# A hybrid decoder block on one core: four more gate blocks by seven products, and all modulation rows out of the retention stage

## The chip, the cores and the metric

The kernel runs on one core of a Trainium2 chip. The metric is the device time of one execution in microseconds. The number before is the median of three runs; a profile of one more execution is read beside it.

## The reference, cut

One decoder block, sequence 1024, width 1024, all in float32. A conditioning vector gives six rows of 1024 modulation values (`c` through SiLU, times `w_ada`). The normed and modulated input goes through one wide projection, and two token mixers run on it side by side; a squared-ReLU MLP follows.

```
mod = silu(c) @ w_ada + b_ada                 # sh1, sc1, g1, sh2, sc2, g2
h = modulate(rms_norm(x, norm1_g), sh1, sc1)
proj = h @ w_in                               # rq, rk, rv, rg, 9 attention parts, 2 gates
ro = retention(rotary(rq), rotary(rk), rv)    # 4 heads, chunks of 128, carried state
ro = group_norm(ro) * gn_g + gn_b
ret_out = (silu(rg) * ro) @ w_ret_out
att_out = dilated attention (3 groups of 4 heads) @ w_att_out
x = x + g1 * ((sigmoid(gate_a) * ret_out + sigmoid(gate_b) * att_out) @ w_o)
x = x + g2 * mlp(modulate(rms_norm(x, norm2_g), sh2, sc2))
return rms_norm(x, norm_f_g)

# retention, one chunk of one head
s = (q @ k.T) * inner_decay
o = s @ v + (q @ state) * q_decay
state = state * chunk_decay + (k * k_decay).T @ v
```

The change is about `rg`, the retention's gate: 2048 columns, 512 a head, in four blocks of 128 a head, sixteen in all.

## The kernel before

Every float32 operand is split into a high and a low half of the type fp32r, and each product is three matmuls (`mm3`: high by low, low by high, high by high) of a stationary 128x128 with a moving 128x512. In the profile these are the lines L210, L212 and L214.

**Blocks by seven products.** The projection stage (`queries_keys`) goes through a list of *pairs*, `PAIRS`; a pair is two blocks of 128 output columns. The contraction, the pair and the sequence are each cut in two, and a scheme of seven products in place of eight is run on the quarters (the class `Blocks`, items `ORDER`). Each product is four row blocks by three matmuls: 84 matmuls a pair. Sums of operands and results are made on VectorE. A pair of kind `r` (retention queries and keys) is followed by the rotary step on VectorE; the kinds `a`, `k`, `g` and `s` have no such step: these are the light pairs. Kind `g` are branch gates, kind `s` the retention's gate; their results go through an activation function and out to DRAM. There are 22 pairs, two of them `s`, the last two.

**Blocks by four products.** The other twelve `rg` blocks are computed in the retention stage, as filling for TensorE: `rg_mm(n)` issues n units, one unit being one of eight contraction blocks of an `rg` block, six matmuls. Eight units end a block, and ScalarE evicts it (L709, SiLU, two halves) into a tile of the ring `E` (five buffers). Its PSUM tiles come from a ring of three, and a block takes two. The table `RG` says how many units each chunk issues.

**The retention stage.** One step per chunk, 8 chunks by 4 heads, in an order written out by hand (`chunk`). On TensorE: `kv` (six matmuls, the state's increment; not in a head's last chunk), the chunk's units but one, `sT` (scores of the next chunk) and `kT` (two transposes of its key; none where the next chunk is a head's last), `o` (nine matmuls), `oT` (four transposes of the chunk before's output), one unit. Beside it VectorE updates the state (L749) and makes its low half (L752), ScalarE copies the scores (L655), makes the state's high half (L756) and evicts the transposes `onT` (L686), VectorE takes the statistics of `o` (L777 to L779), GpSimd makes scale and offset from them in three small steps (L780 to L782, the second a power), and ScalarE writes the scaled output `on` (L790, tile `onm`). `ahead(2)` prepares the weights that the next chunk brings: a cast on ScalarE (L200) and a subtraction on VectorE (L201). From head 1 on VectorE also multiplies an earlier head's output by its gate (L693).

All of the chunk's other PSUM tiles (`kv` twice, `sT`, `kT`, `o`, `oT`) come from one ring of five banks, in this order, so that a tile waits for the readers of the tile five places before it:

```
PS["n"] = 8 if single else 5 if ret else 4
...
return PS["p"].tile(list(shape), F32, tag="s", bufs=PS["n"], name=name)
```

**Modulation rows.** The 48 columns of modulation values are products of a 128x1024 weight tile with the broadcast SiLU of `c`, summed along the row on VectorE. Sixteen are made at the start, 22 by `mod_turn` (two turns a row, a turn with each product of the late pairs and of `values`, from pair 16 on), and the last ten as loads of retention steps (`mod_load`, L467): one in each of chunks 3 to 6 of head 0, two in the first chunk of heads 1, 2 and 3, prepared in the chunk before.

Of the kernel before, what the change touches and what calls it, by code (L numbers as in the profile page):

```python
# [11 lines left out]
F32 = mybir.dt.float32  # L12
# [5 lines left out]
P = 128  # L18
D = 1024
S = 1024  # L20
NK = D // P
H = 4
C = 128
NC = S // C
# [116 lines left out]
def block_kernel(ctx, tc, io, stop=None, dbg=None):  # L141
    nc = tc.nc
# [5 lines left out]
    dram = ctx.enter_context(tc.tile_pool(name="dram", bufs=1, space=bass.MemoryType.DRAM))  # L148
# [20 lines left out]
    def ps_rg(name):  # L169
        return PS["p"].tile([P, 512], F32, tag="rg", bufs=3, name=name)  # L170
# [21 lines left out]
    SH1, SC1, G1, SH2, SC2, G2 = (8 * i for i in range(6))  # L192
# [271 lines left out]
    def mod_prep(i):  # L464

        def prep(raw):
            nc.vector.scalar_tensor_tensor(raw, raw, 1.0, cb, op0=ALU.mult, op1=ALU.mult,  # L467
                                           accum_out=mods[:, i:i + 1])
            nc.vector.tensor_add(mods[:, i:i + 1], mods[:, i:i + 1], vec[:, VC_BADA + i:VC_BADA + i + 1])
        return prep  # L470

    def mod_load(i):
        return io["w_ada"][i], mod_prep(i)

    def proj_mm(ps, w, ks=range(NK)):
        outs = ps if isinstance(ps, list) else [ps[:, 0, :], ps[:, 1, :]]
        for k in ks:
            mm3(outs, wk(w, k), hx[k], k == 0, k == NK - 1)
# [36 lines left out]
    def etile(name, dt=F32):  # L515
        return R["p"].tile([P, 1024], dt, tag="E", bufs=5, name=name)
# [66 lines left out]
    hd = {}  # L583
# [109 lines left out]
        nc.vector.tensor_mul(t, t, hd["srg", h, e][:, 512 * hf:512 * hf + 512])  # L693
        queue.dma_start(y_d[h][:, 2 * (i % 2) + hf, e // 2], t)

    RG = (6, 2, 2, 3, 3, 3, 3, 2), (3, 3, 2, 3, 3, 2, 4, 4), (3, 3, 2, 3, 3, 2, 4, 4), (3, 3, 2, 3, 3, 2, 4, 4)

    def rg_mm(n):

        for _ in range(n):  # L700
            if hd.get("rgk", NK) == NK:
                hd["rgk"], hd["rgw"], hd["rgp"] = 0, hd["rgws"].pop(0), [ps_rg(f"rg{i}") for i in range(2)]
            proj_mm(hd["rgp"], hd["rgw"], [hd["rgk"]])
            hd["rgk"] += 1
            if hd["rgk"] == NK:
                i = hd["rgi"] = hd.get("rgi", -1) + 1
                t = hd["srg", i // 3, i % 3] = etile(f"srg{i // 3}{i % 3}")
                for j, ps in enumerate(hd["rgp"]):
                    nc.scalar.activation(t[:, 512 * j:512 * j + 512], ps, AF.Silu)  # L709

    def rg_out(h, c):

        if c == 6:
            hd["srg", h, 3] = etile(f"srg{h}3")
            nc.sync.dma_start(hd["srg", h, 3], srg_d[h])

    def chunk(h, c, ahead, w=None):
        p = R["p"]
# [7 lines left out]
        if g == 0:  # L726
            rg_mm(2)
            s_kt(0)
            rg_mm(2)
# [9 lines left out]
        if g == 0:  # L739
            s_kt(1)  # L740
        rg_mm(1 if g == 0 else RG[h][c] - (g < NG - 1))
        for i, kv in enumerate(kvs):
            if g == 0:
# [46 lines left out]
        nc.scalar.activation(on, po, AF.Identity, scale=gr[:, 1:2], bias=gr[:, 2:3])  # L790
        hd["o", h, c] = on
        rg_out(h, c)

    def wsplit(ap):
        return ap, split_w
# [2 lines left out]
    va_d = [dram.tile([S, 512], F32, name=f"vad{g}") for g in range(3)]  # L798
    aq_d = {(p, g, a): dram.tile([P, S], F32, name=f"aqd{p}{g}{a}") for p in range(2) for g in range(3) for a in range(2)}
    ak_d = {(p, a): dram.tile([P, S], F32, name=f"akd{p}{a}") for p in range(2) for a in range(2)}  # L800
    srg_d = [dram.tile([P, S], F32, name=f"srgd{h}") for h in range(H)]
    h12_d = [dram.tile([P, 2, 512], F32, name=f"h12d{m}") for m in range(4)]
    xn, wa = [], []

# [330 lines left out]
    def sums_of_h(name, ms=range(4)):  # L1135

        for m in ms:
# [18 lines left out]
            if name != "t4":  # L1156
# [7 lines left out]
    a_pairs = [("a", g, p) for p in range(2) for g in range(3)]  # L1164
    g_pairs = [("g", i) for i in range(len(GATES) // 2)]
    k_pairs = [("k", 2, p) for p in range(2)]
    s_pairs = [("s", i) for i in range(H // 2)]
    PAIRS = [{"r": r_pairs, "a": a_pairs, "g": g_pairs, "k": k_pairs, "s": s_pairs}[i].pop(0)
             for i in "rargrarkrargrarkgagass"]
    MOD0 = 16 * len(ORDER) + 4  # L1170
    NA = len(PAIRS)
    OA = {}
# [74 lines left out]
    gate_d = [dram.tile([P, S], F32, name=f"gated{i}") for i in range(16)]  # L1247
    BA = Blocks("qa", XA, ["x"] * 4 + ["wh", "wl"] * 3, lambda kind: True, a_place, a_two, a_temps, a_out)

    NV = 22  # L1250
    turn = {"n": 0, "i": 0}

    def mod_turn():

        turn["n"] += 1
        while turn["i"] < NV + 2 and turn["n"] > 2 * turn["i"]:
            i = turn["i"]
            turn["i"] += 1
            t = cs[:, i % 2]
            if i > 1:  # L1260
                m = G1 + i - 2
                nc.vector.scalar_tensor_tensor(t, t, 1.0, cb, op0=ALU.mult, op1=ALU.mult, accum_out=mods[:, m:m + 1])
            if i < NV:
                nc.sync.dma_start(t, io["w_ada"][G1 + i])
            if i == NV + 1:
                m = mods[:, G1:G1 + NV]
                nc.vector.tensor_add(m, m, vec[:, VC_BADA + G1:VC_BADA + G1 + NV])

# [176 lines left out]
    RGW, n = [], 0  # L1445
    for g in range(NG):
        RGW += [g - (g > 1)] * (n < 8 * len(RGW) + 1 <= n + RG[g // NC][g % NC])
        n += RG[g // NC][g % NC]
    late_mods = iter(range(G1 + NV, 48))
    for h in range(H):  # L1450
        for c in range(NC):
            steps.add((lambda h, c: lambda ahead, *w: chunk(h, c, ahead, *w))(h, c),
                      ([wsplit(io["w_rg"][RGW.index(NC * h + c)])] if NC * h + c in RGW else []) +
                      [mod_load(next(late_mods)) for _ in range((h > 0 and c == 0) * 2 + (h == 0 and c in (3, 4, 5, 6)))],
                      manual=True)


# [1349 lines left out]
def _cols(w):  # L2807

    k, n = w.shape
    return np.ascontiguousarray(w.reshape(k // P, P, n // P, P).transpose(2, 1, 0, 3)).reshape(n // P, P, -1)  # L2810

def _pairs(w):

    k, n = w.shape
    t = w.reshape(k // 256, 2, P, n // 256, 2, P).transpose(3, 4, 2, 1, 0, 5)
    return np.ascontiguousarray(t).reshape(n // P, P, -1)

def _k4(w):

    k = w.shape[0]  # L2820
    t = w.reshape(k // 512, 4, P, 4, 2, P).transpose(0, 3, 2, 4, 1, 5)
    return np.ascontiguousarray(t).reshape(k // 512 * 4, P, 1024)

def _quads(w):

    k = w.shape[0]
    t = w.reshape(k // 1024, 4, 2, P, 2, 2, 2, P).transpose(0, 6, 2, 4, 3, 5, 1, 7)
    return np.ascontiguousarray(t).reshape(-1, P, 1024)

def _blocks(w):  # L2830

    t = _quads(w).reshape(2, 4, 2, P, 1024).transpose(1, 3, 0, 2, 4)
    return np.ascontiguousarray(t.reshape(4, P, 4, 1024).transpose(0, 2, 1, 3))

def _vblocks(w):

    t = w.reshape(4, 2, P, -1, 2, 512).transpose(4, 1, 2, 3, 0, 5)
    return np.ascontiguousarray(t.reshape(4, P, -1, 1024).transpose(0, 2, 1, 3))

def _vcols(w, width):  # L2840

    n = w.shape[1] // width
    kk = 1024 // width
    t = w.reshape(NK // kk, kk, P, n, width).transpose(3, 0, 2, 1, 4)
    return np.ascontiguousarray(t).reshape(n * (NK // kk), P, 1024)

def _vec(v):
    return np.asarray(v).reshape(-1, P).T
# [37 lines left out]
def pack(x, c, w_ada, b_ada, norm1_g, w_in, rel_bias, ret_gn_g, ret_gn_b,  # L2886
         w_ret_out, w_att_out, w_o, norm2_g, w_ff1, w_ff2, norm_f_g):
    A = np.asarray
    w = A(w_in)[0]
    att = w[:, 6144:10752].reshape(1024, 3, 3, 512)  # L2890
    gates = lambda js: np.concatenate([w[:, 10752 + P * j:10752 + P * j + P] for j in js], axis=1)
    a = {
        "xT": np.ascontiguousarray(A(x)[0].T).reshape(NK, P, S),
        "c": A(c).reshape(1, D),
        "x": A(x)[0].reshape(NC, P, D),
        "w_ada": np.ascontiguousarray(A(w_ada)[0].T).reshape(48, P, D),
        "vec": np.ascontiguousarray(np.concatenate(
            [_vec(A(norm1_g)[0]), _vec(A(norm2_g)[0]), _vec(A(norm_f_g)), _vec(A(b_ada)[0]),
             _vec(A(ret_gn_g)[0]), _vec(A(ret_gn_b)[0])], axis=1)),
        "rel_bias": A(rel_bias),  # L2900
        "w_rq": _pairs(w[:, 0:1024]),
        "w_rk": _pairs(w[:, 1024:2048]),
        "w_rv": _vblocks(w[:, 2048:4096]),
        "w_rg": _cols(w[:, 4096:6144].reshape(1024, 4, 4, P)[:, :, :3].reshape(1024, 1536)),
        "w_rg2": _pairs(w[:, 4096:6144].reshape(1024, 4, 4, P)[:, :, 3].reshape(1024, 512)),
        "w_aq": _pairs(att[:, :, 0].reshape(1024, 1536)),
        "w_ak": _cols(att[:, :2, 1].reshape(1024, 1024)),
        "w_ak2": _pairs(att[:, 2, 1]),
        "w_av": _vcols(att[:, 0, 2], 512),
        "w_av2": _vblocks(att[:, 1:, 2].reshape(1024, 1024)),  # L2910
        "w_gate": _cols(gates(i for c in COVER for i in c)),
        "w_gate2": _pairs(gates(GATES)),
        "w_ret_out": _blocks(A(w_ret_out)[0]),
        "w_att_out": _k4(A(w_att_out)[0]),
        "w_o": _cols(A(w_o)[0]),
        "w_ff1": _pairs(A(w_ff1)[0]),
        "w_ff2": _k4(A(w_ff2)[0, 3072:]),
        "w_ff2s": _quads(A(w_ff2)[0, :3072]),
    }
    a.update(_constants())  # L2920
    return a
# [17 lines left out]
```

## Time and profile before

| | |
|---|---|
| median of three runs | 2165.98 us (2165.3 to 2167.29) |
| profiled execution | 2165.45 us, its span 2163.6 us |
| TensorE busy | 2141.4 us, 10036 matmuls |
| VectorE busy | 1492.1 us |
| ScalarE busy | 983.5 us |
| GpSimd busy | 203.2 us |
| projection pairs | from 180.1 to about 600 us |
| retention stage | about 708.6 to 972.6 us |

A row of the timeline gives the start in us from the span's start, the length, the engine, the line, the operation, the tile written and the tiles read, and in brackets the engine's idle time before it with what ended it. The lengths of matmuls are modelled and overlap; what counts is from one start to the next. In the tables by line "x16: 389/391/476" is the count with the least, median and greatest duration in ns.

### The profile page before, as it was taken

The page shows a single profiled execution, that of the slowest core. Times are in us where ns is not written, and L with a number is a line of the kernel's source. Part 1 is how long each engine was busy: PE and PEld are TensorE (multiplying, and loading weights), DVE is VectorE, ACT ScalarE, POOL GpSimd, SP SyncE. Part 2 cuts the span into 40 slices and gives each one's busy share as a digit, 9 for nine tenths or more (in the row PEclk, how much of TensorE's full clock was granted, in tenths as well). Part 3 has the DMA queues.
Part 4 walks back from the last instruction along what each step waited for, and adds up shares of the span by engine and source line. Part 5 has one row for each costly group of instructions (what it writes and reads, how often), then busy time and mean ns, then how long its engine had stood idle before and what let it go on. Part 6 is the DMA issues. An engine that isn't in the chain of part 4 may idle for free. (4 is left out here: it accounts for less than half of the span.)

```text
span 2163.6 us, 27394 instructions
## 1 busy us (share of the span) xinstructions
PE 2141.4 (99%) x10036; PEld 1782.8 (82%) x10036; DVE 1492.1 (69%) x2320; ACT 983.5 (45%) x1769; POOL 203.2 (9%) x267
## 2 busy tenths in 40 slices
PE   8999999999999999999999999999999999999998
PEld 6888888888888888888888888888778888888887
DVE  6885777777654677666667644777876665977855
ACT  5553322323244566666556635334454455533413
POOL 0001111100001333321110000001000000000003
PEclk9999999999999999999999999999999999999999
DMA  9859998845576655537776366653244435645322
GB/s 383 286 208 301 296 299 248 226 154 202 194 291 241 229 186 180 177 123 213 215 186 188 137 240 221 216 177 129 69 166 161 156 144 195 245 131 175 108 88 78
DMA packets 162931, 425.19 MB, mean 197 GB/s; under 512 B 28261, under 2 KB 56172, under 8 KB 159724
## 3 DMA queue, kind: packets, MB, share of 16 engines
q1 hardware_dynamic: 150456, 374.90, 49.0%
q0 software_dynamic: 9648, 48.24, 10.1%
q8 instruction: 79, 1.29, 0.2%
q10 hardware_dynamic: 2692, 0.30, 0.1%
q14 instruction: 56, 0.46, 0.1%
HBM read 324.13 MB, written 160.32 MB: 224 GB/s over the span
## 5 line engine op out<-in xcount | busy, mean ns | idle before, releaser
L210 PE MATMUL qap<-hh,qaw 128*128 128x512 f32 x264 | 102.7, 389 | 0.0
L212 PE MATMUL qap<-hl,qaw 128*128 128x512 f32 x264 | 102.7, 389 | 0.0
L214 PE MATMUL qap<-hh,qaw 128*128 128x512 f32 x264 | 102.7, 389 | 0.0
L620 POOL TENSOR_TENSOR j<-qk,j 128x512 fp32r<-128x512 f32 x32 | 42.8, 1338 | 400.9 <-ACT j L619 385.5
L2257 POOL TENSOR_TENSOR accnf<-accnf,sqnf 128x256 f32<-128x256 f32 (+1 forms) x18 | 16.6, 923 | 610.0 <-ACT sqnf L2253 610.0
L2361 ACT ACTIVATE a<-a 128x512 f32<-128x512 f32 x48 | 30.3, 631 | 73.7 <-DVE a L2360 73.7
L2569 ACT CAST w2h<-w2s 128x512 fp32r<-128x512 f32 x36 | 22.4, 621 | 78.6 <-DVE w2s L2607 75.7
L214 PEld LDWEIGHTS qap<-hh,qaw 128*128 128x128 f32 x264 | 49.6, 188 | 10.4
L212 PEld LDWEIGHTS qap<-hl,qaw 128*128 128x128 f32 x264 | 49.5, 188 | 10.3
L210 PEld LDWEIGHTS qap<-hh,qaw 128*128 128x128 f32 x264 | 49.5, 188 | 10.3
L267 DVE TENSOR_TENSOR fw<-w1r,fw 128x512 fp32r<-128x512 f32 x48 | 32.9, 688 | 33.6 <-ACT fw L257 33.6
L686 ACT ACTIVATE on<-oT,gnt 128x128 f32<-128x128 f32 x128 | 48.2, 455 | 15.7 <-PE oT L682 15.6
L267 DVE TENSOR_TENSOR qaw<-wa,qaw 128x512 fp32r<-128x512 f32 x66 | 44.0, 686 | 9.6 <-ACT qaw L257 9.6
L2092 DVE TENSOR_TENSOR rwl<-rwl,rwh 128x1024 fp32r<-128x1024 f32 x25 | 30.2, 1220 | 29.1 <-ACT rwh L2122 29.1
L210 PE MATMUL fp<-h2h,fw 128*128 128x512 f32 x128 | 50.0, 390 | 0.0
L1620 ACT ACTIVATE P<-P,ng 128x128 f32<-128x128 f32 (+1 forms) x96 | 41.9, 439 | 17.5 <-DVE ng L1612 17.5
L212 PE MATMUL fp<-h2l,fw 128*128 128x512 f32 x128 | 49.8, 389 | 0.0
L214 PE MATMUL fp<-h2h,fw 128*128 128x512 f32 x128 | 49.8, 389 | 0.0
L210 PE MATMUL roa<-rh,rwl 128*128 128x512 f32 x128 | 49.8, 389 | 0.0
L212 PE MATMUL roa<-rl,rwh 128*128 128x512 f32 x128 | 49.8, 389 | 0.0
L214 PE MATMUL roa<-rh,rwh 128*128 128x512 f32 x128 | 49.8, 389 | 0.0
L656 DVE TENSOR_TENSOR sm<-sm,sT 128x128 f32<-128x128 f32 x32 | 9.2, 288 | 54.6 <-ACT sm L655 54.6
(3092 smaller groups left out, 7214.2 us busy)
## 6 DMA issues: line engine op xcount, KB each, us to landing
v<-vd SPq DMA_DIRECT2D x32, 512.0 KB, 5.1
w1r<-in_w_ff_dram SPq DMA_DIRECT2D x32, 512.0 KB, 4.6
yt<-y POOLq DMA_DIRECT2D x24, 512.0 KB, 7.4
xsd<-as SPq DMA_DIRECT2D x24, 512.0 KB, 2.7
w2r<-in_w_ff2s_dram SPq DMA_DIRECT2D x24, 512.0 KB, 7.0
cossin<-in_w_ada_dram SPq DMA_DIRECT2D x22, 512.0 KB, 3.5
em<-in_w_ada_dram SPq DMA_DIRECT2D x16, 512.0 KB, 10.2
wrvs<-in_w_rv_dram POOLq DMA_DIRECT2D x16, 512.0 KB, 10.1
```

The lines of the kernel that those rows point to most:

```text
L210: nc.tensor.matmul(o, wl, xh, start=first, stop=False, skip_group_check=skip)
L212: nc.tensor.matmul(o, wh, xl, start=False, stop=False, skip_group_check=skip)
L214: nc.tensor.matmul(o, wh, xh, start=False, stop=last, skip_group_check=skip)
L267: nc.vector.tensor_sub(t[:, 512:], src, fv(t[:, :512]))
L620: nc.gpsimd.tensor_sub(t[:, 1], src, fv(t[:, 0]))
L656: nc.vector.tensor_add(sm, sm, ps[:, C:2 * C])
L686: nc.scalar.activation(hd["on", h, c // 4][e][:, c % 4 * C:(c % 4 + 1) * C], po[:, e, :], AF.Identity, scale=gnv[0][:, neg + i:neg + i + 1 ...
L1620: nc.scalar.activation(v, v, AF.Exp, bias=ng[:, blk:blk + 1], accum_out=st[:, g, blk, 2 + a:3 + a])
L2092: nc.vector.tensor_sub(lo, fv(lo), fv(hi))
L2257: (nc.vector if f == 7 else nc.gpsimd).tensor_add(G["acc", key], G["acc", key], sq)
L2361: nc.scalar.activation(o, o, AF.Relu)
L2569: nc.scalar.copy(hi, src)
```

## The change

Four of the twelve `rg` blocks of the retention stage become two more pairs of kind `s`, so that eight of the sixteen are computed by seven products. The table `RG` has eight blocks of units in place of twelve; block 0 and 1 of each head are now computed in the stage, 2 and 3 come back from DRAM in chunks 5 and 6. The ten modulation rows of the retention steps go to `mod_turn`, which makes 32.

```
-    RG = (6, 2, 2, 3, 3, 3, 3, 2), (3, 3, 2, 3, 3, 2, 4, 4), (3, 3, 2, 3, 3, 2, 4, 4), (3, 3, 2, 3, 3, 2, 4, 4)
+    RG = (6, 2, 2, 1, 2, 1, 2, 3), (3, 2, 2, 2, 2, 2, 1, 3), (2, 2, 2, 1, 2, 2, 1, 3), (2, 2, 1, 2, 2, 1, 1, 2)
...
-                t = hd["srg", i // 3, i % 3] = etile(f"srg{i // 3}{i % 3}")
+                t = hd["srg", i // 2, i % 2] = etile(f"srg{i // 2}{i % 2}")
...
-        if c == 6:
-            hd["srg", h, 3] = etile(f"srg{h}3")
-            nc.sync.dma_start(hd["srg", h, 3], srg_d[h])
+        if c in (5, 6):
+            e = c - 3
+            hd["srg", h, e] = etile(f"srg{h}{e}")
+            nc.sync.dma_start(hd["srg", h, e], srg_d[2 * h + e - 2])
...
-    s_pairs = [("s", i) for i in range(H // 2)]
+    s_pairs = [("s", i) for i in range(H)]
     PAIRS = [{"r": r_pairs, "a": a_pairs, "g": g_pairs, "k": k_pairs, "s": s_pairs}[i].pop(0)
-             for i in "rargrarkrargrarkgagass"]
+             for i in "rargrarkrargrarkgagassss"]
...
-    NV = 22
+    NV = 32
...
-    late_mods = iter(range(G1 + NV, 48))
...
-                      ([wsplit(io["w_rg"][RGW.index(NC * h + c)])] if NC * h + c in RGW else []) +
-                      [mod_load(next(late_mods)) for _ in range((h > 0 and c == 0) * 2 + (h == 0 and c in (3, 4, 5, 6)))],
+                      ([wsplit(io["w_rg"][RGW.index(NC * h + c)])] if NC * h + c in RGW else []),
...
-        "w_rg": _cols(w[:, 4096:6144].reshape(1024, 4, 4, P)[:, :, :3].reshape(1024, 1536)),
-        "w_rg2": _pairs(w[:, 4096:6144].reshape(1024, 4, 4, P)[:, :, 3].reshape(1024, 512)),
+        "w_rg": _cols(w[:, 4096:6144].reshape(1024, 4, 4, P)[:, :, :2].reshape(1024, 1024)),
+        "w_rg2": _pairs(w[:, 4096:6144].reshape(1024, 4, 4, P)[:, :, 2:].reshape(1024, 1024)),
```

More of the change, by code (lines that the diff above doesn't have):

```diff
@@ L800, in block_kernel @@
     ak_d = {(p, a): dram.tile([P, S], F32, name=f"akd{p}{a}") for p in range(2) for a in range(2)}
-    srg_d = [dram.tile([P, S], F32, name=f"srgd{h}") for h in range(H)]
+    srg_d = [dram.tile([P, S], F32, name=f"srgd{i}") for i in range(2 * H)]
     h12_d = [dram.tile([P, 2, 512], F32, name=f"h12d{m}") for m in range(4)]
```

## The prediction

> **What bounds the kernel now.** I read the page first, then the busy time by stage, then what TensorE waits for, then the timeline of single chunks.
>
> ```profile
> span 2163.6 us, 27394 instructions
> PE 2141.4 (99%) x10036; PEld 1782.8 (82%) x10036; DVE 1492.1 (69%) x2320; ACT 983.5 (45%) x1769; POOL 203.2 (9%) x267
> ```
>
> TensorE is busy for 99% of the span, but the ends of matmuls are modelled, so I look at the two stages that the change touches: the last pairs of the projection stage, and the retention stage with all its 32 chunks.
>
> ```profile
> core 0: us, PE busy (x) PEld busy (x) DVE busy (x) ACT busy (x) POOL busy (x), PEclk, DMA share, GB/s
> 500.00:600.00 100.00, 100.00 (x443) 82.81 (x442) 71.71 (x111) 31.79 (x53) 0.00 (x0) 1.00 0.58 201
> 708.60:972.60 264.00, 264.00 (x1313) 220.71 (x1312) 178.87 (x394) 168.05 (x368) 90.37 (x123) 1.00 0.54 175
> ```
>
> ```profile
> engine line waited for: us in total, times, longest us
> PE pb L444 <- DMA onehot<-in_onehot_dram: 5.6, 2, 4.3
> ```
>
> In the first row 443 matmuls issue in 100 us: 0.226 us for one of 512 columns, at a granted clock of 1.00. The second row is the retention stage: TensorE never idle, VectorE 68% busy, ScalarE 64%. The table of TensorE's waits has its largest row at the kernel's start (above), and no row at all between 600 and 980 us. So in both stages the time is the number of matmuls by 0.226 us, as long as nothing else comes late. The forecast is about whether that stays so in chunks with less filling.
>
> **The change part by part.**
>
> *Matmuls.* A gate block by four products is one weight block of 16 matmuls on each of three lines, 48; a light pair (two blocks) is seven products of four row blocks by three, 84.
>
> ```profile
> L210 PE MATMUL rg<-hh,raw_5340l x16: 389/391/476, 708.3 to 726.2; 128*128 128x512 f32 x16
> L210 PE MATMUL qap<-hh,qaw x264: 389/389/389, 180.3 to 595.8; 128*128 128x512 f32 x132
> ```
>
> The first row is one of the twelve blocks. In the second, 264 on one line over 22 pairs are 12 a pair: the three products with unsummed weights. The retention stage loses four blocks (192 matmuls, 43.4 us), the projection stage gains two pairs (168, 38.0 us): 24 fewer, **-5.4 us** if TensorE stays full in both.
>
> *Added pairs.* The two new pairs are of the kind that already ran last, inside the first windows row: VectorE at 71.7% beside a full TensorE. I cost them at nothing beyond their matmuls. If that cover were gone, 19 us of pair at 72% VectorE would have to slip by 28% before it showed. The four more gate blocks go out to and come back from DRAM on SP's queue, 0.5 MB each; the loads stand in chunks 5 and 6 of a head and are used in chunks 4 and 6 of the next, and behind them in the queue stand only loads that run three chunks ahead of use. Nothing.
>
> *Modulation rows.* Ten go from the retention stage to the turns beside the light pairs and in the first values, one in two turns, as the other 22 do now.
>
> ```profile
> L467 DVE SCALAR_TENSOR_TENSOR raw<-raw,cb 128x1024 f32<-128x1024 f32 x10 | 12.2, 1217 | 0.0
> 841.00 1.46 POOL L781 TENSOR_TENSOR gr<-gr,ct 128x1 f32<-128x1 f32 x1
> 815.76 0.54 POOL L781 TENSOR_TENSOR gr<-gr,ct 128x1 f32<-128x1 f32 x1
> 807.11 1.00 POOL L781 TENSOR_TENSOR gr<-gr,ct 128x1 f32<-128x1 f32 x1
> ```
>
> They free 12.2 us of VectorE there. They also stand in front of GpSimd's small power: 1.46 us beside a row's product (841.00), 0.54 to 1.00 us without one. This saves nothing now, since TensorE does not wait there, but it makes the chunk's end 0.5 to 0.9 us earlier where a row stood. [...]
>
> *Thinner chunks.* This is where it is decided. A unit is six matmuls, 1.36 us; a chunk had mostly three, it now has two, and eight chunks have one. The chain of a chunk (statistics on VectorE, three steps on GpSimd, then ScalarE writes the scaled output `on`) does not get shorter, and it gives back the PSUM bank of `o`, one of five in a ring, which the next chunk's key transpose `kT` takes (or its own `o` when the chunk after it is a head's last, since that one has no `kT`). Here is a chunk with two units, head 1 chunk 2, from the end of the chunk before it; the last two rows are from chunks 5 and 6:
>
> ```profile
> 788.83 0.40 PE L214 MATMUL o<-v,smh 128*128 128x512 f32 x1
> 790.90 0.39 PE L210 MATMUL kv<-v,kl 128*128 128x512 f32 x1
> 791.09 1.06 ACT L200 CAST raw_6201h<-raw 128x1024 fp32r<-128x1024 f32 x1
> 792.03 0.80 ACT L790 ACTIVATE onm<-o,gr 128x512 f32<-128x512 f32 x1
> 792.04 0.39 PE L214 MATMUL kv<-v,kh 128*128 128x512 f32 x1
> 792.18 1.23 DVE L201 TENSOR_TENSOR raw_6201l<-raw,raw_6201h 128x1024 fp32r<-128x1024 f32 x1 [1.01 <-ACT raw_6201h L200]
> 793.93 1.28 DVE L749 SCALAR_TENSOR_TENSOR state<-state,kv 128x512 f32<-128x512 f32 x2
> 794.03 0.40 PE L648 MATMUL kT<-ct,qk 128*128 128x128 f32 x2
> 796.12 0.40 PE L214 MATMUL o<-v,smh 128*128 128x512 f32 x1
> 797.43 1.50 ACT L686 ACTIVATE on<-oT,gnt 128x128 f32<-128x128 f32 x4
> 798.18 0.39 PE L210 MATMUL kv<-v,kl 128*128 128x512 f32 x1
> 798.82 1.09 ACT L709 ACTIVATE srg<-rg 128x512 f32<-128x512 f32 x2
> 799.55 0.62 PE L210 MATMUL rg<-hh,raw_6201l 128*128 128x512 f32 x2
> 800.42 0.78 ACT L790 ACTIVATE onm<-o,gr 128x512 f32<-128x512 f32 x1 [0.52 <-POOL gr L782]
> 802.67 0.40 PE L648 MATMUL kT<-ct,qk 128*128 128x128 f32 x2
> 825.01 0.78 ACT L790 ACTIVATE onm<-o,gr 128x512 f32<-128x512 f32 x1 [0.52 <-POOL gr L782]
> 828.62 0.45 PE L210 MATMUL o<-stateh,j 128*128 128x512 f32 x1
> ```
>
> ```profile
> L709 ACT ACTIVATE srg<-rg x24: 593/611/621, 727.5 to 971.0; 128x512 f32<-128x512 f32 x24
> ```
>
> And this is what a wait costs beyond its length:
>
> ```profile
> 1235.92 1.02 ACT L2004 ACTIVATE g<-gate 128x1024 f32<-128x1024 f32 x1
> 1236.99 0.73 PE L210 MATMUL ao<-ah,raw_10314l 128*128 128x512 f32 x2 [0.73 <-ACT g L2004]
> 1237.56 0.39 PE L212 MATMUL ao<-al,raw_10314h 128*128 128x512 f32 x1
> ```
>
> ScalarE ends at 1236.94, TensorE restarts 0.05 later, and its first two matmuls then take 0.57 us in place of 0.45: about 0.17 us for a restart.
>
> (a) `kT` in one-unit chunks (head 0 chunks 3 and 5, head 2 chunk 3, head 3 chunks 2 and 5). `on` ended at 792.83, `kT` came at 794.03: slack 1.20. One unit less takes 1.36, so it is 0.16 short, 0.33 with the restart. Ends: 0 (`on` 0.4 earlier) and 0.8. I take 0.4 by five: 2.0.
>
> (b) Chunk 6 of heads 1 to 3, four units before, one now; there `o` takes the bank. `on` ended at 825.79, `o` came at 828.62: slack 2.83, three units less are 4.08, short by 1.25, with the restart 1.4. In these rows, as in the new head 1, weights had been prepared one chunk earlier, and that makes `on` late (see d) by 1.1; in heads 2 and 3 this falls elsewhere: 1.4 - 1.1, taken as 0.4 each. Sum 2.2, ends 0.5 and 4.
>
> (c) A finished gate block is evicted on ScalarE after the four `onT` copies; the next block's second product needs the first evicted bank. In the rows that is free at 799.43 (798.82 and one copy of 0.61) and needed at 799.78 (the block's second matmul), with six `kv` matmuls (1.36 us) lying between the blocks. Now blocks end in chunk 6 of heads 0 and 2, and a head's last chunk has no `kv`: needed at 798.42, 1.0 late, 1.2 with the restart. In head 0, which has no final multiply on VectorE, I take 0.8. In head 2 the chunk before prepares weights: in the rows above that (1.06 on ScalarE, then 1.23 on VectorE) made the state update start at 793.93, when `kv` was out at 792.43, 1.5 late, and a one-unit chunk cannot make this up: 2.7 at most, I take 2.4. The three block ends with a `kv` behind them have at most 0.2 of slack by the rows; I take 0.3, 0.3 and (one unit, head 3) 0.7. Sum 4.5, ends 1.5 and 6.5.
>
> (d) Behind a chunk that prepares weights, `on` ends late: 5.1 us after the last matmul of `o` was out (796.12 to 801.20) against 4.0 us in the chunk before (788.83 to 792.83), and it still waited for GpSimd. Up to `kT` at 802.67, with three units, that left 1.47; two leave 0.1. Three such places besides those counted, at 0.3: 0.9. And GpSimd's power varies by half a microsecond (0.54 to 1.00): 0.9 more over all thin chunks. Sum 1.8, ends 0 and 4.
>
> Waits: 2.0 + 2.2 + 4.5 + 1.8 = 10.5 us, ends 2 and 18.5. With -5.4: **+5.1 us**. The profiled execution took 2165.45 us, 0.5 below the median of 2165.98; on it the sum gives 2170.6, on the median **2171.1 us**, 0.24% slower. Differences under 0.2% (4.3 us) I call the same: about what a measurement of this kernel can tell from no change.
>
> **The rivals.**
>
> *The lag does not build up (faster).* Then each `on` ends 4.0 us or less behind `o`, as in the chunk ahead of the rows, not 5.1: ten rows and four weight splits have left VectorE's queue. (a) falls to nothing, (c) and (d) nearly; TensorE waits under 1 us in all. Time 2165.98 - 5.4 + 0.6 = 2161.2. It decides at a lag of about 3.8 us in the one-unit chunks (4.0 less the 0.16 that (a) is short). For it: the 12.2 us, and that no wait shows now. Against it: the late chunk of the rows has no modulation row in it, and six chunks still prepare weights. Chance 0.12.
>
> *Waits as I list them, but smaller (same).* If the silu waits are 1 us each at most and (d) is nothing, the waits are 5 to 9 us: 2165.5 to 2169.6. Chance 0.30.
>
> *VectorE becomes the bound.*
>
> ```profile
> DVE sm L656 <- ACT sm L655: 54.6, 31, 3.4
> ```
>
> VectorE's 178.87 us are 5.6 a chunk, and it stands 1.8 us a chunk waiting for ScalarE's copy of the scores (54.6 by 31). If that idle time cannot shrink, since VectorE works in order, its period is 7.4 us against 7.28 of a two-unit chunk (790.90 to 798.18) and 5.9 of a one-unit chunk: 1.5 more in eight chunks, 0.1 in twelve, 13 us of waits in place of 10.5, and with (c) on top of them 17: 2165.98 - 5.4 + 17 = 2178. For it: the order of its queue. Against it: the idle time is what TensorE's surplus leaves over now. Chance 0.11.
>
> ```profile
> PEclk9999999999999999999999999999999999999999
> ```
>
> *Something else late.* The new pairs wait, each once or twice for a product of 1.22 us in VectorE's queue: 2 to 5 us, 2173 to 2176. Against it the first windows row. Or a wait lowers TensorE's clock: ten matmuls at 0.45 us cost 2.3 us more, 2173.4 for one such place. Against it: after 4.3 us of one wait at the start the page's clock line has no lower digit, and I expect none over 2.7. [...] Chance 0.03 for both.
>
> *That the change does not do what it says* I exclude: the units of the new lists sum to 64, eight blocks of eight.
>
> **How the numbers follow.** Forecast (waits 9.8 to 14.5 us) 0.44, own range 2170.4 to 2175. Slower by over 0.2%: 0.44 + 0.11 + 0.03 = 0.58; same 0.30; faster 0.12. The range runs from 2161.5, which takes in half of the faster rival, to 2178, the middle of VectorE's.
>
> **What would show it.** In the changed profile: 10012 matmuls in all if no record is missing; retention about 264 - 43.4 + 10.5 = 231 us long; TensorE waits there, most of it on `rg` for `srg` and on `kT` and `o` for `onm`; the longest where head 2's last chunk begins; none in the pairs; power steps on GpSimd of 1.0 us or less. Wrong if the table of waits has still no row in that stage (faster rival), if `kv` or `o` wait for VectorE's `state` or `statel` all along (VectorE's rival), or if the pairs show waits.

## The result, and the profile after

The changed kernel takes 2170.17 us (median of 11 runs, 2168.78 to 2172.45) against 2166.05 us for the kernel before (11 runs, 2164.66 to 2167.71): a ratio of 1.0019, 95% interval 1.0012 to 1.0027. It is slower, by 4.1 us, with an interval that lies on both sides of the 0.2% that the prediction called the same. The profiled execution took 2172.45 us and is the slowest of its 11 runs.

The page of the changed kernel, its rows for the span and the engines:

```profile
span 2170.7 us, 27411 instructions
PE 2142.1 (99%) x10012; PEld 1780.4 (82%) x10012; DVE 1506.7 (69%) x2338; ACT 987.0 (45%) x1781; POOL 201.9 (9%) x267
```

24 matmuls fewer, as counted. The same two stages as before by windows (the last 100 us of the pairs, then retention, from 1 us before the first `rg` to the first `ak`), and under them the table of TensorE's waits between 600 and 1000 us, where before had no row:

```profile
538.00:638.00 100.00, 100.00 (x442) 82.82 (x442) 71.71 (x112) 34.04 (x58) 0.00 (x0) 1.00 0.56 194
747.40:980.30 232.90, 227.11 (x1129) 186.99 (x1128) 162.37 (x362) 157.93 (x356) 89.91 (x123) 0.99 0.54 175
...
PE rg L210 <- ACT srg L709: 3.4, 3, 2.4
PE o L210 <- ACT onm L791: 1.8, 5, 0.8
PE rg L210 <- DVE vr L1378: 0.6, 1, 0.6
PE va L212 <- DVE vwlTrue L1341: 0.3, 1, 0.3
```

The pairs still run without a gap. Retention has waits now, on the evicted gate blocks and on `onm`, and its mean granted clock is 0.99. The table of waits shows less than what is lost: it counts from the modelled end of the matmul before, and short waits and a lower clock are not in it. So I measure stages from the first matmul of one tile to the first of the next, against the kernel before (`qap` to `vc` are the pairs, `vc` to `rg` the first values, `rg` to `ak` retention, `ak` to `gate` the first part of attention; us, profiled executions):

| kernel | to `qap` | pairs | first values | retention | to `gate` | rest |
|---|---|---|---|---|---|---|
| before, in full | 180.30 | 418.88 | 109.15 | 264.59 | 58.19 | 1132.53 |
| changed | +1.21 | +38.08 | +0.75 | -32.61 | -0.01 | -0.38 |
| weights earlier | +0.22 | +38.08 | +1.69 | -35.67 | -0.01 | -0.48 |
| rows only | -0.19 | 0.00 | +1.91 | +1.79 | 0.00 | +0.12 |
| blocks only | -0.02 | +38.08 | -0.35 | -26.60 | 0.00 | +0.08 |
| faster turns | +0.53 | +42.59 | -0.33 | -32.64 | -0.01 | +2.07 |
| two ends | -0.27 | +38.08 | +1.87 | -37.47 | -0.04 | +0.05 |
| other units | +2.04 | +38.08 | +0.41 | -35.90 | +1.58 | +0.31 |
| other units, even rows | +0.74 | +38.23 | +1.73 | -35.27 | +2.08 | +0.83 |
| other units, other bank | -0.04 | +38.08 | +0.53 | -37.65 | -0.01 | +1.30 |

The first and the last column hold work that no version changes: they vary by 1 to 2 us from one execution to the next, and so much is not read into a single profile. The pairs cost what 168 matmuls cost, +38.08. Retention should have given -43.4 and gave -32.6: 10.8 us are lost in it. These are the places.

**The longest wait**, head 2, from chunk 6 to chunk 7 (timeline; start, length, engine, line, operation, in brackets the idle time and what ended it), and the clock around it (windows; the third figure from the end is the granted clock, the first after the window's length is TensorE's busy time):

```profile
915.75 0.40 PE L210 MATMUL rg<-hh,raw_6601l 128*128 128x512 f32 x1
917.91 1.09 ACT L709 ACTIVATE srg<-rg 128x512 f32<-128x512 f32 x2
918.57 0.57 PE L210 MATMUL rg<-hh,raw_6601l 128*128 128x512 f32 x1 [2.42 <-ACT srg L709]
918.94 1.05 PE L212 MATMUL rg<-hl,raw_6601h 128*128 128x512 f32 x2
919.79 1.05 PE L214 MATMUL rg<-hh,raw_6601h 128*128 128x512 f32 x2
920.64 1.05 PE L210 MATMUL rg<-hh,raw_6601l 128*128 128x512 f32 x2
```

```profile
915.46:918.87 3.41, 0.99 (x4) 0.51 (x4) 3.18 (x8) 3.07 (x8) 2.17 (x3) 1.00 1.07 400
918.87:922.28 3.41, 3.41 (x9) 2.65 (x8) 0.24 (x1) 0.92 (x2) 0.84 (x2) 0.50 0.89 278
```

The first matmul of the new block is in at 915.75, the second needs a bank that ScalarE is still to evict: 2.82 us from start to start in place of 0.23. Behind it two matmuls take 0.85 us from start to start (918.94 to 919.79, to 920.64), 0.43 each in place of 0.23: nine matmuls run wholly or in part in the window of 3.41 us at a granted clock of 0.50, 1.7 us more. Only the profiled execution shows this stretch. How many of the other ten had one stays open: a run's mean granted clock, known to three digits (0.999 in five, 0.998 in six), can't tell, since the profile of *two ends* below has 0.998 too and no such stretch.

**A late `on`**, head 1 chunk 1 (timeline): the chunk ahead prepares weights.

```profile
818.13 0.95 POOL L782 TENSOR_TENSOR gr<-gr,ct 128x1 f32<-128x1 f32 x1
818.87 1.23 DVE L201 TENSOR_TENSOR raw_5717l<-raw,raw_5717h 128x1024 fp32r<-128x1024 f32 x1 [0.20 <-ACT raw_5717h L200]
819.16 0.99 POOL L783 TENSOR_TENSOR gr<-gr 128x1 f32<-128x1 f32 x1
820.18 0.78 ACT L791 ACTIVATE onm<-o,gr 128x512 f32<-128x512 f32 x1 [1.34 <-POOL gr L783]
821.02 0.51 PE L210 MATMUL o<-stateh,j 128*128 128x512 f32 x1 [0.27 <-ACT onm L791]
```

GpSimd's last step takes 0.99 us, nearly all of it beside VectorE's subtraction; by itself it is 0.19 (the experiment below has the range). ScalarE idles 1.34 us for it, and `o`, not `kT`, waits for the bank.

**No wait in chunk 6**, head 1 (timeline): `o` starts a microsecond before the `onm` of chunk 5 does.

```profile
856.00 0.45 PE L210 MATMUL o<-stateh,j 128*128 128x512 f32 x1
857.01 0.78 ACT L791 ACTIVATE onm<-o,gr 128x512 f32<-128x512 f32 x1 [1.08 <-POOL gr L783]
```

It has another bank. In the built program the `o` tiles of head 1 lie in these banks, chunk 0 to chunk 7:

```
1 1 1 1 1 1 4 2
```

The text ahead of the prediction has the ring of five go round in order; it doesn't. By the placements of the built program a new tile gets the bank that has been free the longest. In this head each `o` comes back to the bank of the `o` before it as long as the chunk has a `kT`; in chunk 6 there is none, and `o` gets another bank.

**The start of retention** (timeline): the second `rg` bank holds the last value product.

```profile
748.57 0.69 DVE L1378 TENSOR_TENSOR vr<-vr,vc 128x512 f32<-128x512 f32 x1 [0.59 <-PE vc L214]
749.31 0.50 PE L210 MATMUL rg<-hh,raw_5630l 128*128 128x512 f32 x1 [0.56 <-DVE vr L1378]
```

Here too it is the placement. With 24 pairs the last `vc` lies in bank 7, which `rg` takes; with 22 it lay in bank 0, which is needed only later. It costs 0.8 us with the restart; the wait of 0.6 us is there in every version with 24 pairs.

### The profile page after: what moved, and what is told of

Same layout as the page of the kernel before. It is cut to its first block, busy times and chain, and to the rows that moved or that the text cites. A ratio compares the mean times of both kernels' runs of the same rounds, so it can differ in the third digit from the quotient of the medians.

```text
span 2170.7 us, 27411 instructions
## 1 busy us (share of the span) xinstructions
PE 2142.1 (99%) x10012; PEld 1780.4 (82%) x10012; DVE 1506.7 (69%) x2338; ACT 987.0 (45%) x1781; POOL 201.9 (9%) x267
## 5 line engine op out<-in xcount | busy, mean ns | idle before, releaser
L210 PE MATMUL qap<-hh,qaw 128*128 128x512 f32 x288 | 112.0, 389 | 0.0
L212 PE MATMUL qap<-hl,qaw 128*128 128x512 f32 x288 | 112.0, 389 | 0.0
L214 PE MATMUL qap<-hh,qaw 128*128 128x512 f32 x288 | 112.0, 389 | 0.0
L210 PEld LDWEIGHTS qap<-hh,qaw 128*128 128x128 f32 x288 | 54.1, 188 | 11.3
L212 PEld LDWEIGHTS qap<-hl,qaw 128*128 128x128 f32 x288 | 54.1, 188 | 11.2
L214 PEld LDWEIGHTS qap<-hh,qaw 128*128 128x128 f32 x288 | 54.1, 188 | 11.2
L2256 POOL TENSOR_TENSOR accn<-accn,sqn 128x512 f32<-128x512 f32 x12 | 15.5, 1293 | 322.8 <-ACT sqn L2252 322.8
```

The costliest lines, as they stand in the source:

```text
L210: nc.tensor.matmul(o, wl, xh, start=first, stop=False, skip_group_check=skip)
L212: nc.tensor.matmul(o, wh, xl, start=False, stop=False, skip_group_check=skip)
L214: nc.tensor.matmul(o, wh, xh, start=False, stop=last, skip_group_check=skip)
L2256: (nc.vector if f == 7 else nc.gpsimd).tensor_add(G["acc", key], G["acc", key], sq)
```

## The experiments

Each was measured beside the kernel before, whose median was 2166.08 us beside the first four, 2165.64 us beside the next three and 2166.10 us beside the last. Behind each median stand the range of its runs, the ratio to the kernel before and the ratio's 95% interval.

### Weights earlier

```
+    RGW[6] -= 1
     for h in range(H):
         for c in range(NC):
```

The seventh block's weights are prepared in head 2 chunk 4, not 5, so that the chunk ahead of the longest wait has none.

> The weights of the seventh gate block are prepared one chunk earlier than in the changed kernel (head 2 chunk 4 in place of chunk 5); nothing else differs. Theory (the long wait in front of head 2's last chunk comes from that preparation standing in front of a one-unit chunk on VectorE and ScalarE): the 2.6 us wait of rg for the gate's eviction falls to about 1 us, and with it the stretch of matmuls at half clock behind it disappears; about 3 us less in a profile that had the stretch, 2 us less in the median, so 2168. Rival (the wait is the eviction's own length and the missing state product): the wait stays at 2 us or more and the time at 2170.

Measured: 2171.06 us (2168.5 to 2173.1) against 2166.08; 1.0017, 1.0008 to 1.0025. The table of waits, and the window around the place of the longest wait:

```profile
PE rg L210 <- ACT srg L709: 2.5, 3, 1.5
PE o L210 <- ACT onm L791: 1.4, 5, 0.4
...
915.00:925.00 10.00, 8.50 (x43) 6.79 (x42) 5.20 (x14) 6.11 (x15) 5.58 (x8) 1.00 0.72 239
```

The longest wait went from 2.4 to 1.5 us, and the clock stays at 1.00 behind it; `o` waits 0.4 less in all, and retention is 3.1 us shorter. So the weights prepared just ahead of the eviction were 0.9 us of that wait, and behind the shorter wait no half clock followed. What is left, 1.5 us, lies between the theory (about 1) and the rival (2 or more). The expected 2168 us was missed: the median is no lower than the changed kernel's, though the profiled execution took 2169.24 us, so this run alone doesn't settle the gain.

### Rows only

```
-    NV = 22
+    NV = 32
...
-                      [mod_load(next(late_mods)) for _ in range((h > 0 and c == 0) * 2 + (h == 0 and c in (3, 4, 5, 6)))],
```

The kernel before with the ten rows moved and all blocks as they were.

> The kernel before with only the modulation rows moved: all 32 late rows by turns beside the light pairs and the first values, none in the retention stage, gate blocks as before. Theory (the rows make VectorE late in the first values, where TensorE then waits): 0.5 to 2 us more waits in the first values, none in the retention stage, 2166.5 to 2168. Rival (the rows are free there and the 1.6 us of waits in the changed kernel's first values are chance or come from elsewhere): 2166 and the same 0.3 us of waits there as before.

Measured: 2169.99 us (2168.13 to 2176.82), 1.0018, 1.0010 to 1.0026. Its waits:

```profile
PE ak L210 <- ACT on L686: 1.6, 1, 1.6
PE vc L212 <- DVE vwl L1338: 1.5, 1, 1.5
```

This was not free. In the first values `vc` waits for the low half of its operand: +1.9, as the theory had it. The chain ahead of that wait shows where the rows come in (timeline; ScalarE in the kernel before, then ScalarE and VectorE here):

```profile
645.27 0.60 ACT L1372 ACTIVATE vo<-va 128x512 fp32r<-128x512 f32 x1 [3.31 <-DMA vd<-vo]
...
648.36 0.60 ACT L1372 ACTIVATE vo<-va 128x512 fp32r<-128x512 f32 x1 [5.44 <-DMA vd<-vo]
649.60 1.22 DVE L1262 SCALAR_TENSOR_TENSOR cossin<-cossin,cb 128x1024 f32<-128x1024 f32 x1
```

A row's product takes 1.22 us of VectorE in this chain, and ahead of it ScalarE stands 5.4 us until a store of values has landed, where it stood 3.3 us in the kernel before. Each row also brings a load of 0.5 MB on the queue of these stores: 15 between 590 and 700 us in place of 5. And at the start of attention `ak` waits for the transposes of the last output but one: +1.8, where the theory had no wait; with it the median is 2 us above the expected 2166.5 to 2168. That wait goes with the placement, not with the rows as work: in this build these transposes lie in bank 4, and `ak` always takes banks 4 and 5. In the kernel before and in the changed one bank 4 has long been free there.

### Blocks only

```
-    NV = 32
+    NV = 22
...
+    late_mods = iter(range(G1 + NV, 48))
```

The changed kernel with the ten rows back in the retention steps.

> The changed kernel with the ten modulation rows put back into the retention steps; the gate blocks as changed. Theory (rows in VectorE's queue make the end of a chunk later, and thin chunks have no cover): waits in the retention stage 2 to 4 us above the changed kernel's 8, at the head boundaries and before head 0's last chunk; in the first values 1.3 us fewer. Together 2171 to 2173. Rival (the rows are covered in thin chunks too): 2168.5, the first values' gain alone.

Measured: 2175.92 us (2175.69 to 2176.97), 1.0043, 1.0030 to 1.0056. Waits, then GpSimd's two last steps by line (least, median, greatest duration in ns):

```profile
PE o L210 <- ACT onm L791: 6.0, 7, 1.3
PE rg L210 <- ACT srg L709: 4.2, 2, 2.4
...
L782 POOL TENSOR_TENSOR gr<-gr,ct x32: 538/979/1537, 759.2 to 985.3; 128x1 f32<-128x1 f32 x32
L783 POOL TENSOR_TENSOR gr<-gr x32: 192/193/1164, 759.9 to 986.3; 128x1 f32<-128x1 f32 x32
```

With thin chunks the rows cost 6.0 us of retention that they did not cost in thick ones; `o` waits 6.0 us for `onm` in place of 1.8, and the power reaches 1.54 us. The theory was right in kind, and its 2171 to 2173 us too low. In the changed kernel the power stays at 1.00:

```profile
L782 POOL TENSOR_TENSOR gr<-gr,ct x32: 539/932/1003, 761.6 to 981.5; 128x1 f32<-128x1 f32 x32
```

So the two parts of the change need each other: the rows had to go for the chunks to get thin. The first values are back to 0.35 us under before.

### Faster turns

```
-        while turn["i"] < NV + 2 and turn["n"] > 2 * turn["i"]:
+        while turn["i"] < NV + 2 and 2 * turn["n"] > 3 * turn["i"]:
```

Two rows in three products, so that all are made before the first values begin.

> The changed kernel with a modulation row every turn and a half in place of every second turn, so that all 32 are done before the first values begin. Theory (the waits in the first values are the rows' doing): the waits there fall from about 1.9 us to the 0.3 us of before, no wait in the pairs, 2168.5 to 2169. Rival (VectorE beside the pairs is then too full): new waits among the pairs of 1 us or more, time 2170 or above.

Measured: 2176.34 us (2174.44 to 2177.62), 1.0044, 1.0032 to 1.0056.

```profile
PE qap L210 <- DVE qat L296: 3.3, 3, 1.5
PE gate L210 <- DVE raw_10241l L201: 1.8, 1, 1.8
...
538.00:638.00 100.00, 96.75 (x424) 78.91 (x422) 76.27 (x122) 32.13 (x56) 0.00 (x0) 1.00 0.63 216
```

The first values no longer wait (-0.33), but the pairs do, +4.5 us, at 76% VectorE in this window. The rival came true. The cover that the forecast named for the pairs is real and thin: `qap` waits for the addition L296. At the longest of these waits three rows, 3.2 us apart, stand ahead of the additions in VectorE's order, the last at 594.78 us, and TensorE's last matmul before the wait starts at 595.46. *Even rows* below has three such rows at the same place, at 74% VectorE in the same window, but the last starts at 591.90 us, and the pairs lose 0.15 us: where the last row falls decides, more than VectorE's share. The second line above, in the attention stage, is 2.0 us of the last column that I don't explain.

### Two ends

```
-    RG = (6, 2, 2, 1, 2, 1, 2, 3), (3, 2, 2, 2, 2, 2, 1, 3), (2, 2, 2, 1, 2, 2, 1, 3), ...
+    RG = (6, 2, 2, 1, 2, 1, 3, 2), (3, 2, 2, 2, 2, 2, 1, 3), (2, 2, 2, 1, 2, 2, 2, 2), ...
```

> The changed kernel with two of its lists altered by one unit each: head 0 ends in 3, 2 in place of 2, 3, and head 2 in 2, 2, 2, 2 in place of 2, 2, 1, 3. Blocks 2 and 6 are then finished one unit earlier, and the next block's first unit stands in the same chunk, not at the head of the last chunk that has no `kv`. All else as in the changed kernel (2169 to 2172 us). Theory (the two waits at these places are the finished block's eviction, and the slow stretch behind the longer one is the clock's answer to it): the row `rg` for `srg` falls from 3.4 us to under 1 us, no stretch at half clock, `o` for `onm` stays near 1.8 us or rises by up to 0.5; 2166.0 to 2168.0 us. Rival (ScalarE and VectorE are late by a fixed amount there, and TensorE pays it at the next place): `rg` for `srg` falls but `o` for `onm` rises by 2 us or more; 2169 us or above.

Measured: 2167.80 us (2166.26 to 2168.42) against 2165.64; 1.0007, 0.9998 to 1.0016. The table of waits has no row for `srg` any more:

```profile
PE o L210 <- ACT onm L791: 2.6, 5, 1.2
PE va L210 <- ACT va L1387: 1.3, 1, 1.3
```

`rg` for `srg` is gone, `o` for `onm` has 0.8 more (up to 0.5 was expected), and the granted clock is 1.00 from 900 to 940 us, where the changed kernel's stretch at 0.50 lay: retention has -37.47 in place of -32.61. With two units moved by one chunk the median lies 2.2 us above the kernel before in place of 4.1, inside the expected range; the interval now holds no change. The rival (2 us or more given back at the next place) is out.

### Other units

```
+    RG = (6, 3, 2, 2, 1, 2, 2, 1), (2, 3, 2, 1, 2, 2, 2, 2), (2, 3, 2, 1, 2, 3, 1, 2), (2, 3, 2, 1, 2, 1, 1, 1)
```

> The changed kernel with other lists of units: (6, 3, 2, 2, 1, 2, 2, 1), (2, 3, 2, 1, 2, 2, 2, 2), (2, 3, 2, 1, 2, 3, 1, 2), (2, 3, 2, 1, 2, 1, 1, 1). They have the same 64 units, but no block ends just ahead of a chunk without `kv`, no one-unit chunk is next to another but for the last three, and a chunk with three units stands behind most that prepare weights. Theory (the 10 us of waits in retention come from where blocks and thin chunks fall, not from too little TensorE work in all): TensorE's waits in retention under 4 us, no stretch at half clock, first values unchanged with 1.6 us more than before; 2162 to 2165 us, faster than both kernels. Rival (VectorE and ScalarE need their 7.3 us a chunk whatever the order): the waits stay at 8 us or more, only under other names; 2168 to 2171 us.

Measured: 2171.69 us (2170.28 to 2172.98), 1.0026, 1.0016 to 1.0037. Neither theory. Waits, the place (ScalarE, then TensorE), and the clock there:

```profile
PE ak L210 <- ACT onm L791: 4.6, 1, 4.6
PE o L210 <- ACT onm L791: 1.0, 3, 0.5
...
976.71 0.78 ACT L791 ACTIVATE onm<-o,gr 128x512 f32<-128x512 f32 x1 [1.40 <-POOL gr L783]
977.54 1.09 PE L210 MATMUL ak<-hh,raw_7282l 128*128 128x512 f32 x2 [4.60 <-ACT onm L791]
...
974.31:977.72 3.41, 0.18 (x1) 0.18 (x2) 1.48 (x4) 2.01 (x5) 1.31 (x3) 1.00 0.67 205
977.72:981.13 3.41, 3.41 (x9) 2.63 (x10) 1.83 (x2) 0.70 (x1) 0.44 (x1) 0.50 0.30 74
```

Inside retention the expectation holds: 1.0 us on `onm`, nothing on `srg`. At its end `ak` stands 4.6 us for the very last `onm`, and a stretch of 3.41 us at a granted clock of 0.50 follows. In this build the last `o` lies in bank 4, which `ak` takes. In the changed kernel it lies in bank 1. A table of counts had changed a placement at the other end of the stage.

### Other units, even rows

```
-    def mod_turn():
+    def mod_turn(k=1):
...
-                mod_turn()
+                mod_turn(2 - 2 * (ORDER.index(n) % 2))
```

The units of the version above, and with them its bank; the rows go with the first, third, fifth and seventh of a pair's products.

> The lists of the kernel with other units, and the modulation rows beside pairs at every second of a pair's seven products, always the first, third, fifth and seventh, in place of every second product counted through; 30 of the 34 turns are then done with the pairs, in place of 26, and never two rows in the two products ahead of the additions on which the next pair's bank waits. Theory (the first values wait because eight rows are left to them, and the pairs waited at three rows in four products because of two rows next to each other ahead of these additions): no wait in the pairs, the wait of `va` in the first values gone or halved, the wait of `rg` for `vr` of 0.6 us still there; 1 to 1.5 us less than with the other units alone, 2161 to 2163.5 us. Rival (VectorE has no room for more than 26 rows beside the pairs): `qap` waits for `qat`, 1 us or more in several pairs; no gain or 1 to 3 us more than with the other units alone.

Measured: 2172.82 us (2171.68 to 2176.36), 1.0035, 1.0022 to 1.0047.

```profile
PE ak L210 <- ACT onm L791: 4.6, 1, 4.6
PE va L210 <- ACT va L1387: 1.1, 1, 1.1
...
972.58:975.99 3.41, 1.16 (x8) 0.75 (x6) 2.02 (x3) 3.41 (x8) 0.00 (x0) 1.00 0.71 231
975.99:979.40 3.41, 1.06 (x3) 0.87 (x4) 0.95 (x3) 1.83 (x3) 1.31 (x3) 0.50 0.71 231
979.40:982.82 3.42, 3.42 (x10) 2.64 (x9) 1.68 (x2) 0.00 (x0) 0.60 (x1) 0.50 0.35 80
```

(The windows are for the last section.) The time, 1.1 us above the units alone, misses the expected 1 to 1.5 us below them. The half on the pairs was right in its result: four rows in seven products in fixed places cost the pairs 0.15 us, not 4.5. The half on the first values was wrong: `va` still waits with four turns left to them in place of eight. And the kernel with two ends, whose code in this stage is the changed kernel's, had 1.3 us there against none in the changed kernel's profile: the wait varies between executions of one code. Behind it stands a load: ScalarE waits for the weights `vwlTrue` 7.4 to 7.7 us in the three profiles in which `va` waits (*weights earlier*, *two ends* and this one), and 5.1 to 6.5 us in the seven in which it doesn't. The shortest, 5.1 and 5.2 us, are those of *blocks only* and *faster turns*, which leave as few rows as before, or none, to the first values. What of the later landing is the rows' loads and what is chance stays open.

### Other units, other bank

```
-    ... (2, 3, 2, 1, 2, 1, 1, 1)
+    ... (2, 2, 2, 1, 2, 1, 1, 2)
```

> The kernel with other units, with head 3 in (2, 2, 2, 1, 2, 1, 1, 2) in place of (2, 3, 2, 1, 2, 1, 1, 1): one unit is moved from its second chunk to its last. By this the last `o` of the retention lands in PSUM bank 3 in place of bank 4, by the order in which banks come free; the first `ak` of the attention takes banks 4 and 5 in every version. Theory (the 4.8 us at the start of the attention, and the 3.4 us at half clock behind them, come from `ak` and the last `o` sharing a bank): the row `ak` for `onm` of 4.6 us goes, the clock stays whole, TensorE's waits in retention stay under 4 us; 6 to 8 us less than with the other units, 2163.5 to 2166 us, level with the kernel before or a little faster. Rival (the last chunk is too thin for its chain, whatever the bank): `ak` still waits, 3 us or more with one unit more; 2168 to 2171 us.

Measured: 2167.62 us (2164.76 to 2168.42) against 2166.10; 1.0003, 0.9994 to 1.0012.

```profile
PE o L210 <- ACT onm L791: 2.9, 5, 1.1
...
973.84 0.70 PE L210 MATMUL ak<-hh,raw_7282l 128*128 128x512 f32 x2
976.21 0.78 ACT L791 ACTIVATE onm<-o,gr 128x512 f32<-128x512 f32 x1 [0.85 <-POOL gr L783]
```

`ak` starts 2.4 us before the last `onm` does, and the mean granted clock of the profiled execution is 0.998, with the other bank 0.997: the median lies 1.5 us above the kernel before, with the other bank 6.1. One unit more in the last chunk could not have covered 4.6 us (a unit is 1.36), so this was the bank. It missed its expected 2163.5 to 2166 by 1.6 us; `o` waits 2.9 us for `onm` in place of 1.0. No version beats the kernel before: with the best lists retention still loses 5.8 of its 43.4 us (0.8 of them at its start), and 5.4 was all that there was to win.

## Why the prediction was right, step by step

It forecast 2171.1 us in a range of 2161.5 to 2178, and 2170.17 came, 0.9 below. The mechanism was right: the thin chunks leave TensorE waiting on ScalarE's eviction and on `onm`, and this eats the 5.4 us twice over. The sum came out nearer than its terms. By the prediction's own line of 0.2% (4.3 us) the 4.1 us measured still count as the same, to which it gave 0.30, and the median falls between the range it gave its forecast (2170.4 to 2175) and that of the rival with smaller waits (2165.5 to 2169.6).

| step | forecast, us | measured in the profile, us |
|---|---|---|
| matmuls | -5.4 | -5.4 (24 fewer; pairs +38.08) |
| added pairs | 0 | 0 |
| rows moved | 0 | first values +0.75 here, +1.9 alone |
| (a) `on` in one-unit chunks | 2.0 | 1.8 |
| (b) chunk 6 of heads 1 to 3 | 2.2 | 0 |
| (c) gate blocks' eviction | 4.5 | 4.1 |
| (d) late `on` elsewhere | 1.8 | 1.9 |
| half clock | 0 | 1.7, in the profiled execution |
| last `vc` in `rg`'s bank | 0 | 0.8 |
| end of the stage, to `ak` | 0 | 0.3 |

Retention's measured terms are the distances from the first `o` matmul of one chunk to that of the next, above those of the kernel before, with 1.36 us for each unit taken out. They sum to 10.6; the 10.8 that the stage lost holds 0.2 more, spread over the other chunks.

- **(c) was right in its places too.** Head 0's eviction cost 0.8 (forecast 0.8), head 2's 2.6 (2.4), head 3's 0.7 (0.7); the other block ends with a `kv` behind them, two of them at 0.3 each in the forecast, cost nothing. *Two ends* shows it from the other side: without the two ends the waits and the half clock are gone.
- **(a) and (d) were right in sum, not in place.** (a) was taken as 0.4 by five; head 2 chunk 3 alone cost 1.0, the two of head 3 cost 0.3 and 0.5, the two of head 0 nothing. It is `o` that waits, 0.2 us behind `kT`, because `o` and not `kT` takes that bank. A restart, 0.17 us in the forecast, costs 0.03 at `o` (0.34 us to the next matmul, 0.31 without a wait).
- **(b) failed** at the sentence "there `o` takes the bank". It came from a ring that goes round in order. The ring gives out the bank that has been free the longest, and in chunk 6 that is another one. The 2.2 us never were, and neither was the lower end of 0.5.
- **"Modulation rows ... as the other 22 do now" failed**: *rows only* cost 1.9 us in the first values. The sum priced the rows' products in VectorE's queue beside the pairs; it left out the first values behind them, where a row's 1.22 us stands in the chain, and the rows' loads on the queue of that stage's stores and weights. What it says of GpSimd held: power steps of 1.00 us at most without rows (the changed kernel), up to 1.54 with them (*blocks only*). The last step shows the same spread, 0.99 us beside the weights' subtraction and 0.19 by itself; why a step on GpSimd is longer beside VectorE, no run here shows.
- **A lower clock behind a wait was a rival, and it came.** An idle time of 2.42 us was followed by 3.41 us at a granted clock of 0.50. The prediction gave this rival 0.03 (with late pairs) and 2.3 us; it came on top of the forecast, at 1.7. Against its ten matmuls at 0.45 us the profile shows nine, those wholly in the stretch at 0.43. Its reason against it, that the page's clock line has no lower digit after 4.3 us of one wait, was a misreading: a digit stands for a slice of 54 us, and the changed kernel's line is all nines too, in spite of its 3.41 us at half clock. In the kernel before, the first 512-column matmuls behind the waits at the start were slow (timeline):

```profile
11.50 3.47 PE L876 MATMUL av<-wv0wh,hh 128*128 128x512 f32 x8 [1.70 <-ACT hh L413]
14.81 2.01 PE L876 MATMUL av<-wv0wh,hl 128*128 128x512 f32 x8
```

Eight take 3.31 us from start to start, 0.41 each, and the next eight, to 16.66, take 0.23 each. The record of granted clocks begins only at 14.46 us, so a table of windows shows 1.00 there.

- **The rivals.** *The lag does not build up* is out by the table of waits. *Waits as I list them, but smaller* needed 5 to 9 us in retention; it lost 10.8, and would have lost about 9.1 without the half clock. *VectorE becomes the bound* is out: no row of `kv` or of `o` waiting for `state` all along.
- So the near total is in part luck: (b) was 2.2 us too much, the half clock and the bank at the start 2.5 too little. With either alone the forecast would have been 2 to 3 us off, still inside its range. And the profiled execution, from which the terms come, is 7.0 us slower than the profile before (1.2 of it ahead of the pairs, 0.75 in the first values), where the medians differ by 4.1.

## What to carry to other kernels

Work that fills one engine's gaps has a second value, as distance between a release and its next use: before it is moved to a cheaper form elsewhere, list for each chunk what becomes due earlier, and put the thin chunks where no eviction and no weight preparation ends just ahead. Where tiles come from a ring, look up the placement in the built program instead of counting places: changing a table of counts, or moving rows, changed which tile lies in a bank that a later stage takes first, for 0.8 to 4.6 us (with the half clock behind it, 1.7 us by a stretch of 3.41, 6 us and more). And when both parts of a change are meant to help each other, run each alone: here the blocks alone cost 9.8 us, the rows alone 3.9 (about half of it a placement), and both together 4.1.

## What was not expected of the hardware

A TensorE idle time of 2.42 us (2.82 from start to start) was followed by a stretch of 3.41 us at a granted clock of 0.50 in the profile of the changed kernel; the idle time of 2.4 us at the same wait was followed by one of 3.4 us in those of *blocks only* and of *faster turns* as well. Times of 1.5 us (*weights earlier*), 1.6 (*rows only*) and 1.8 (*blocks only* and *faster turns*) were not. Behind 4.6 us the stretch was 3.41 us in *other units* and 6.83 in *even rows*.

These are single profiles. Between 170 and 1400 us they have no idle time of TensorE between 1.8 and 2.4 us. They do not show why a stretch at half clock follows one idle time and not another, what made it twice as long behind one wait of 4.6 us as behind the other, or how often a wait of 2.4 us is followed by one.
